# Strassen's seven products for the gate projections of a two-block kernel, with x loaded a second time

## The chip, the cores and the metric

The kernel runs on one NeuronCore of a Trainium2 chip. The metric is the device time of one execution in microseconds. PE is the matrix engine, DVE the vector engine, ACT the scalar engine, POOL the general engine (GpSimd), SP the queue that issues most loads.

## The reference, cut to what matters

Two transformer blocks, one after the other, on 512 tokens of width 1024 in float32. The change is in the first:

```python
h = rms_norm(x, norm_mix_pre[l])
proj = h @ w_in[l]
q, k, v, u, gates = jnp.split(proj, splits, axis=-1)
y_a = chunk_band_attention(q, k, v, rel_bias[l]) @ w_attn_out[l]
y_b = multiscale_pool(u, w_pool_group[l], pool_scale[l]) @ w_pool_out[l]
g_a, g_b = jnp.split(jax.nn.sigmoid(gates + b_gate[l]), N_BRANCH, axis=-1)
mix = (g_a * y_a + g_b * y_b) @ w_o[l]
x = x + rms_norm(mix, norm_mix_post[l])
```

`gates` is 512 tokens by 2048, so its transpose is 16 tiles of 128 channels by 512 tokens.

## The kernel before, in words

Everything is held with channels on the 128 partitions and tokens along the free dimension. A float32 product is made of three matrix products of numbers with short mantissas: each operand is split into a high part (`split_hi`, a copy on ACT that rounds) and a low part (`split_lo`, source minus high part, on DVE), and `mm3` (L411) adds high·high, high·low and low·high in one PSUM bank. A 128x512 output over 1024 input channels is 8 such triples, 24 matmuls of 512 columns (`gemm`, L416).

Weights come in a fixed order (`weight_order`, L66). `fetch` (L366) loads one tile from SP, `split_next` (L377) splits it into one of four `whi`/`wlo` buffers, `take` (L406) hands it to the product. The order of all instructions is settled at build time: the class `Issue` (L107) holds an estimate of each engine's time; every operation goes through `Engine` (L231, so all rows of the profile name that line) and is written into its engine's queue when the estimate says that its turn has come. Small tasks (evacuations, softmax steps, splits) are generators that `step` (L191) resumes between two matmuls. On the chip each engine then works through its queue strictly in order.

The part in question runs as follows. `hhi`/`hlo` are the eight split tiles of `x` times `g_mix`; the tiles `xs` of x stay in SBUF for the residual. After q, k and v, attention (`attn_item`, `attn_values`) runs as small tasks between the products of `w_u`, whose four tiles go through `pooling` (L863): DVE and ACT make moving sums, three matmuls `t<-phi,whi`, `t<-plo,whi`, `t<-phi,wlo` follow, and the result is split into `ph`/`pl`. Then for each m of 8 (L931): two gate tiles (`w_g`, 24 matmuls of 512 columns each), `gate` (L908) multiplies by the row norm `rb1` and takes the tanh; the products `pa` and `pb` (`w_ap`, 12 matmuls each) of attention and pooling follow; `mixing` (L915) joins them into `mxh`/`mxl`. `project_norm` (L575) multiplies these by `w_o`, and its `Seam` adds the result to `xs`. PSUM has 3 banks "mm", 2 "s", 3 "t" (L252).

```python
V.tensor_tensor(lo, src, hi.bitcast(F32), op=ALU.subtract)     # split_lo, L356
V.tensor_tensor(t, ps, rb1, op=ALU.mult)                       # gate, L910
V.tensor_tensor(gt[0], gt[0], gt[1], op=ALU.add)               # mixing, L923
```

Of the kernel before, what the change touches and what calls it, by code (L numbers as in the profile page):

```python
# [10 lines left out]
F32R = mybir.dt.float32r  # L11
# [15 lines left out]
BIG = 1e30  # L27
NACT = 75
WBUF = 1088
NS = 4  # L30

UNITS = ["a6", "a10", "a4", "a1", "a8", "a7", "a3", "a5", "a2", "a9", "q1", "v0", "a0", "q0",
# [33 lines left out]
def weight_order():  # L66

    o = []

    def add(name, i=None, a=0, b=None):  # L70
        o.append((name, i, a, b))

    for hp in range(4):
        add("w_qk", 2 * hp)
        add("w_qk", 2 * hp + 1)
        if hp == 0:
            for i in range(4):
                add("w_v", i)
    add("w_pg")
    for i in range(4):  # L80
        add("w_u", i)
    for m in range(KD):
        add("w_g", 2 * m)
        add("w_g", 2 * m + 1)
        add("w_ap", m)
    for m in range(KD):
        add("w_o", m)
    for i in range(2 * MF):
        add("w_up", i)
# [17 lines left out]
class Issue:  # L107
# [11 lines left out]
    @staticmethod  # L119
    def cells(ap):  # L120
        if ap.space == bass.MemoryType.DRAM:
            return (0,)
        w = ap.ap[0][0]
        a = ap.offset % w
        return range(a // 64, (a + sum(max(st, 0) * (n - 1) for st, n in ap.ap[1:])) // 64 + 1)

    def ready(self, *aps):
        t = 0.0
# [108 lines left out]
def kernel(ctx, tc, aps, out, dbg=None):  # L237
# [26 lines left out]
    def wbuf(tag, n):  # L264

        t = wp.tile([P, WBUF], F32R, tag=tag, name=tag, bufs=4)
        return t[:, :n]
# [29 lines left out]
    def grab_now(tag):  # L297
        until(lambda: tokens[tag])
        until(lambda: tokens[tag][0][0] <= iss.now + LEAD)
        return psum(tag)  # L300

    def free(ps):
        tag, b = bank.pop(ps.name)
        tokens[tag].append((iss.mark, b))
        tokens[tag].sort()

    def after(*aps):
        while iss.ready(*aps) > iss.now + LEAD:
            yield
# [44 lines left out]
    def split_lo(src, hi, lo, scale=None):  # L354
        if scale is None:
            V.tensor_tensor(lo, src, hi.bitcast(F32), op=ALU.subtract)  # L356
        else:
            V.scalar_tensor_tensor(lo, src, scale, hi.bitcast(F32), op0=ALU.mult, op1=ALU.subtract)


    plan = weight_order()
    raws, done = [], []
    early = {("w_up", i) for i in range(NS - 1)} | {("w2_a", int(u[1:])) for u in UNITS[:NS - 1]}
    npos = {"fetch": 0, "split": 0, "taken": 0}

    def fetch():  # L366
        if npos["fetch"] == len(plan):
            return
        name, i, a, b = plan[npos["fetch"]]
        npos["fetch"] += 1  # L370
        src = aps[name] if i is None else aps[name][i]
        n = (src.shape[-1] if b is None else b) - a
        raw = wp.tile([P, n], F32, tag="w32", name="w32", bufs=2)
        load(nc.sync, raw, src[:, a:a + n])
        raws.append(((name, i, a, b), raw, n))

    def split_next():  # L377
        while not raws:
            yield
        key, raw, n = raws.pop(0)  # L380
        yield from after(raw)
        if key[:2] in early:
            hi = [act("wh", F32R) for _ in range(2)]
            lo = [act("wl", F32R) for _ in range(2)]
            for i in range(2):
                split_hi(raw[:, 512 * i:512 * i + 512], hi[i])
                yield
                split_lo(raw[:, 512 * i:512 * i + 512], hi[i], lo[i])
        elif key[0] == "w_out" and key[1] < NPART:

            a, b = NFIRST * P, (8 - NFIRST) * P
            keep = act("wk", F32R), act("wk", F32R)
            hi = [wbuf("whi", a), keep[0][:, :b]]
# [5 lines left out]
        else:  # L399
            hi = wbuf("whi", n)  # L400
            lo = wbuf("wlo", n)
            split_hi(raw, hi)
            yield
            split_lo(raw, hi, lo)
        done.append((key, hi, lo))
        fetch()  # L406

    def take(name, i=None, a=0, b=None):
# [3 lines left out]
        until(lambda: done)  # L412
# [424 lines left out]
    for hp in range(4):  # L837
# [7 lines left out]
        if hp == 0:  # L845
# [9 lines left out]
            spawn(attn_scores())  # L855
            spawn(attn_values())


    plh, pll = [None] * 4, [None] * 4
    wg = weights("w_pg")  # L860

    def pooling(g, ps):
        u = act("u")  # L863
        yield from after(ps)
        V.tensor_tensor(u, ps, rb, op=ALU.mult)
        free(ps)
        yield
        win = u
        for i in range(g + 1):
            s = 1 << i  # L870
            nxt = act("win")
# [23 lines left out]
        plh[g], pll[g] = hi, lo  # L895

    for g in range(4):
        w = weights("w_u", g)
# [6 lines left out]

    rb1 = rb

    def gate(t, ps, col):  # L908
        yield from after(ps)
        V.tensor_tensor(t, ps, rb1, op=ALU.mult)  # L910
        free(ps)
        yield
        A.activation(t, t, AF.Tanh, bias=col, scale=0.5)

    def mixing(m, gt, pa, pb):  # L915
        yield from after(pa, *gt)
        V.scalar_tensor_tensor(gt[0], gt[0], 1.0, pa, op0=ALU.add, op1=ALU.mult)
        free(pa)
        yield from after(pb)
        V.scalar_tensor_tensor(gt[1], gt[1], 1.0, pb, op0=ALU.add, op1=ALU.mult)  # L920
        free(pb)
        yield 0
        V.tensor_tensor(gt[0], gt[0], gt[1], op=ALU.add)  # L923
        yield
        hi, lo = act(f"mh{m}", F32R), act(f"ml{m}", F32R)
        split_hi(gt[0], hi, 0.5)
        yield
        split_lo(gt[0], hi, lo, 0.5)
        mxh[m], mxl[m] = hi, lo

    for m in range(KD):  # L931
        gt = []
        for b in range(2):
            w = weights("w_g", 2 * m + b)
            ps = grab_now("mm")
            gemm(ps, w, hhi, hlo)
            t = act("gate")
            spawn(gate(t, ps, hb[:, 8 * b + m:8 * b + m + 1]))
            gt.append(t)
# [6 lines left out]
        spawn(mixing(m, gt, pa, pb))  # L946
    sn = project_norm(lambda m: [(("w_o", m), range(KD))], mxh, mxl, "g_mix_post", 3, "g_ffn")


# [903 lines left out]
```

## Time and profile before

| | |
|---|---|
| time, median of 3 runs (lowest to highest) | 1023.47 us (1023.25 to 1023.51) |
| the profiled execution: its own time, its span | 1022.24 us, 1020.5 us |
| PE busy | 998.9 us, 98% of the span |
| DVE busy | 694.0 us, 68% |
| ACT busy | 495.9 us, 49% |
| POOL busy | 74.8 us, 7% |
| mean granted TensorE clock | 0.994 |
| loads and stores | 97.19 MB, mean 95 GB/s |

The profiled execution took 1.7 us more than its span, and 1.23 us less than the median of the three runs. A busy share says how long an engine had something in work, and matmuls overlap, so PE's share does not say how near PE is to its peak; the distance from one matmul's start to the next does.

### The profile page before, as it was taken

The numbers are of one execution on the slowest core, as the hardware profiler recorded it, in microseconds if no ns is written. First come the engines' busy times: TensorE is split into PE (matmuls) and PEld (weight loads), VectorE is DVE, ScalarE is ACT, GpSimd is POOL, SyncE is SP. The second block draws the span as 40 slices with busy tenths as digits, with TensorE's granted clock in tenths as the row PEclk, the third lists the DMA queues.
The fourth block names the chain that finished last, engine by engine and source line by source line (L and its number), as shares of the span: only waits on it lengthen the run. The fifth ranks groups of instructions, "written<-read, shape, count | busy, mean of one in ns | idle before, by whom it ended". The sixth has DMA issues, their size and how long they took to land.

```text
span 1020.5 us, 15112 instructions
## 1 busy us (share of the span) xinstructions
PE 998.9 (98%) x5718; PEld 845.8 (83%) x5718; DVE 694.0 (68%) x1429; ACT 495.9 (49%) x1032; POOL 74.8 (7%) x146
## 2 busy tenths in 40 slices
PE   8999999999999999999999999999999989999898
PEld 7977678888888888888888888898899978889786
DVE  6688874444348997766776422369885787999972
ACT  6577543233354554344444322244466675575970
POOL 2000000000002100000001000014000450001001
PEclk9999999999999999999999999999999998999999
DMA  7422122232241233222224333331433440114112
GB/s 260 143 73 81 55 83 90 97 103 94 92 128 38 80 107 99 90 101 103 87 100 119 103 89 92 114 104 28 180 101 110 132 94 22 35 43 134 61 63 83
DMA packets 40345, 97.19 MB, mean 95 GB/s; under 512 B 12160, under 2 KB 16528, under 8 KB 40272
## 3 DMA queue, kind: packets, MB, share of 16 engines
q1 hardware_dynamic: 37392, 87.53, 27.1%
q0 software_dynamic: 2736, 8.66, 2.5%
q8 instruction: 45, 0.74, 0.3%
q14 instruction: 28, 0.23, 0.1%
q10 hardware_dynamic: 144, 0.03, 0.0%
HBM read 90.29 MB, written 5.91 MB: 94 GB/s over the span
## 4 chain that ended last, share of the span: by engine, by line
PE 80%; DVE 13%; DMA 3%; ACT 2%; issue 1%; POOL 1%; SPq 0%; DVEq 0%
PE mm L231 71%; PE t L231 5%; PE s L231 3%; DVE nl L231 2%; DVE x L231 2%; DVE wlo L231 1%; DVE f L231 1%; DVE rsq_t L231 1%; DVE e L231 1%; DMA w<-w_up 1%; DMA T<-dx 1%; DMA w<-w_qk 1%; POOL xt L231 1%; DVE acc L231 1%; POOL cb L231 1%
## 5 line engine op out<-in xcount | busy, mean ns | idle before, releaser
L231 DVE TENSOR_TENSOR wlo<-w,whi 128x1024 fp32r<-128x1024 f32 (+4 forms) x153 | 180.6, 1186 | 63.3 <-ACT whi L231 63.2
L231 PE MATMUL mm<-nh,whi 128*128 128x512 f32 x448 | 176.3, 393 | 0.0
L231 PE MATMUL mm<-nh,wlo 128*128 128x512 f32 x448 | 176.0, 393 | 0.0
L231 PE MATMUL mm<-nl,whi 128*128 128x512 f32 x448 | 175.6, 392 | 0.0
L231 ACT ACTIVATE whi<-w 128x1024 fp32r<-128x1024 f32 (+4 forms) x153 | 154.8, 1018 | 42.6 <-DMA w<-w_dn 22.0
L231 PEld LDWEIGHTS mm<-nh,wlo 128*128 128x128 f32 x448 | 84.2, 188 | 17.0
L231 PEld LDWEIGHTS mm<-nh,whi 128*128 128x128 f32 x448 | 84.2, 188 | 16.9 <-issue 0.4
L231 PEld LDWEIGHTS mm<-nl,whi 128*128 128x128 f32 x448 | 84.2, 188 | 16.7
L231 PE MATMUL mm<-l,whi 128*128 128x512 f32 x208 | 82.4, 396 | 0.0
L231 PE MATMUL mm<-h,whi 128*128 128x512 f32 x208 | 82.3, 396 | 0.0
L231 PE MATMUL mm<-h,wlo 128*128 128x512 f32 x208 | 82.3, 395 | 0.0
L231 PE MATMUL mm<-gh,whi 128*128 128x512 f32 (+1 forms) x198 | 72.5, 366 | 0.0
L231 PE MATMUL mm<-gh,wlo 128*128 128x512 f32 (+1 forms) x198 | 72.4, 366 | 0.0
L231 PE MATMUL mm<-gl,whi 128*128 128x512 f32 (+1 forms) x198 | 72.4, 366 | 0.0
L231 ACT ACTIVATE y<-hu,par 128x512 f32<-128x512 f32 x40 | 32.4, 810 | 63.5 <-DVE hu L231 63.5
L231 DVE SCALAR_TENSOR_TENSOR y<-hu,par,y 128x511 f32<-128x511 f32 x80 | 59.9, 749 | 1.4
L231 POOL TENSOR_TENSOR acc<-acc,sq 128x256 f32<-128x256 f32 (+1 forms) x31 | 26.3, 847 | 418.0 <-ACT sq L231 417.9
L231 PE MATMUL mm<-wlo,nh 128*128 128x256 f32 (+1 forms) x192 | 55.5, 289 | 0.0
L231 PE MATMUL mm<-whi,nl 128*128 128x256 f32 (+1 forms) x192 | 55.3, 288 | 0.0
L231 PE MATMUL mm<-whi,nh 128*128 128x256 f32 (+1 forms) x192 | 55.1, 287 | 0.0
L231 DVE TENSOR_TENSOR hu<-mm,nb 128x512 f32<-128x512 f32 x40 | 27.6, 691 | 39.5 <-PE mm L231 39.5
L231 DVE TENSOR_TENSOR acc<-acc,sq 128x512 f32<-128x512 f32 (+1 forms) x21 | 14.3, 683 | 48.7 <-ACT sq L231 48.5
(344 smaller groups left out, 2209.8 us busy)
## 6 DMA issues: line engine op xcount, KB each, us to landing
w<-w_up SPq DMA_DIRECT2D x44, 512.0 KB, 3.5
w<-w_g SPq DMA_DIRECT2D x16, 512.0 KB, 3.5
w<-w_dn SPq DMA_DIRECT2D x16, 448.0 KB, 3.5
w<-w_a SPq DMA_DIRECT2D x12, 512.0 KB, 3.5
w<-w_ap SPq DMA_DIRECT2D x8, 512.0 KB, 3.5
w<-w_o SPq DMA_DIRECT2D x8, 512.0 KB, 3.4
w<-w_dn SPq DMA_DIRECT2D x8, 512.0 KB, 3.6
w<-w_z SPq DMA_DIRECT2D x8, 512.0 KB, 3.8
```

Of the source, the lines that this page charges most:

```text
L231: return f(*args, **kw)
```

## The change

For each m, the two gate tiles (output channels b = 0, 1) and the two halves of the tokens are taken as a 2 by 2 matrix of 128x256 quarters, and the 1024 input channels as two halves of four tiles. Seven products of 12 matmuls of 256 columns (`strassen`) take the place of eight. The operands are sums of quarters:

- of the activations, once: `forms_of` makes T1 to T4 out of x for each of 4 pairs of input tiles: 2 scaled copies on ACT, 4 differences of 128x256 on POOL, then 2 splits of 128x512 (ACT, DVE). It is started as a task after v.
- of the weights, for each m: `split_next` loads four tiles `rw` of 128x512, POOL makes S1, S2, S3 (and later S4) of 128x512, `split_pair` splits seven quarters (ACT, DVE) into halves of the four weight buffers.
- of the products, for each m: `Sums` copies the first out of PSUM on ACT and adds the other six in seven additions of 128x256 on DVE into the tiles C11 to C22, which are the two gate tiles.

The multiplication by `rb1` now reads SBUF in place of PSUM, `mixing` adds on POOL in place of DVE, and x is loaded again into eight tiles from POOL's queue behind the loop, since the first copies' room is used. `cells` follows tiles in pieces of 16 columns in place of 64; `no_slot` keeps at most four weight buffers in use.

```diff
@@ weight_order
     for m in range(KD):
-        add("w_g", 2 * m)
-        add("w_g", 2 * m + 1)
+        add("w_g", 2 * m, "pair", 2 * m + 1)
         add("w_ap", m)
@@
+    def forms_of(forms_, src, hi, lo, scale):
...
+        for j in range(n):
+            x, y, g, gy = src(j), src(j + n), scale(j), scale(j + n)
+            xg, yg, t, u = (act("tf") for _ in range(4))
+            A.activation(xg, x, AF.Copy, scale=g)
+            A.activation(yg, y, AF.Copy, scale=gy)
+            yield
+            t1, t2, t3, t4 = t[:, half], t[:, other], u[:, half], u[:, other]
+            G.tensor_tensor(t1, xg[:, other], xg[:, half], op=ALU.subtract)
+            G.tensor_tensor(t2, yg[:, other], t1, op=ALU.subtract)
+            G.tensor_tensor(t3, yg[:, other], xg[:, other], op=ALU.subtract)
+            G.tensor_tensor(t4, yg[:, half], t2, op=ALU.subtract)
+            yield
+            for src_, names in ((t, ("T1", "T2")), (u, ("T3", "T4"))):
+                th, tl = act("th", F32R), act("tl", F32R)
+                split_hi(src_, th)
+                yield
+                split_lo(src_, th, tl)
...
@@ split_next
+        if key[2] == "pair":
...
+            s1, s2 = act("sw"), act("sw")
+            G.tensor_tensor(s1, b1, b2, op=ALU.add)
+            G.tensor_tensor(s2, s1, a1, op=ALU.subtract)
+            G.tensor_tensor(b1, a1, b1, op=ALU.subtract)
...
+            yield from split_pair(w, a1, a2, b1, b2, s1, s2)
@@
+    def split_pair(w, a1, a2, b1, b2, s1, s2):
...
+        yield from split("A11", a1)
+        yield from split("S2", s2)
+        G.tensor_tensor(s2, a2, s2, op=ALU.subtract)
+        yield from split("S3", b1)
+        yield from split("A12", a2)
+        yield from split("S1", s1)
+        yield from split("A22", b2)
+        yield from split("S4", s2)
+
+    FORM = {"A11": "B11", "S2": "T2", "S3": "T3", "A12": "B21", "S1": "T1", "A22": "T4", "S4": "B22"}
+
+    def strassen(w, forms, tags, out):
+        for (a, b), tag in zip(FORM.items(), tags):
+            until(lambda: a in w and b in forms)
+            (whi, wlo, slot), (xh, xl) = w[a], forms[b]
+            n = len(xh)
+            ps = grab_now(tag)[:, :256]
+            for j in range(n):
+                mm3(ps, whi[:, csl[j]], wlo[:, csl[j]], xh[j], xl[j], j == 0, j == n - 1)
+            slot["left"] -= 1
+            spawn(out(a, ps), True)
@@ Sums
+            V.tensor_tensor(self.t[name], ps, self.t[other], op=ALU.add)
...
+            if a == "A11":
+                A.activation(self.t["m1"], ps, AF.Copy)
+                self.have.add("m1")
+            else:
+                for name, other in {"S2": (("v", "m1"),), "S3": (("a", "v"),), "A12": (("C11", "m1"),),
+                                    "S1": (("w", "v"), ("C22", "a")), "A22": (("C21", "a"),),
+                                    "S4": (("C12", "w"),)}[a]:
+                    yield from self.add(name, ps, other)
@@ mixing
-        V.tensor_tensor(gt[0], gt[0], gt[1], op=ALU.add)
+        G.tensor_tensor(gt[0], gt[0], gt[1], op=ALU.add)
@@
+    def gated(m, gt, gdone):
+        def done(last):
+            t, col = (gt[1], 8 + m) if last == "A22" else (gt[0], m)
+            V.tensor_tensor(t, t, rb1, op=ALU.mult)
+            yield
+            A.activation(t, t, AF.Tanh, bias=hb[:, col:col + 1], scale=0.5)
...
+        strassen(w[0], hforms, ("s", "mm", "s", "mm", "s", "mm", "s"), Sums(*gt, gated(m, gt, gdone)).out)
...
+    xs[:] = [act(f"x{k}") for k in range(KD)]
+    for k in range(KD):
+        load(nc.gpsimd, xs[k], aps["xT"][k])
```

What the change moves in the queues stands in three places. POOL, from the last loads of attention's bias `rel` on (`acc<-acc,sq` belongs to the norm after `w_o`); before:

```order
L281 DMA rel_977<-rel 128x512
L281 DMA rel_979<-rel 128x512
L281 DMA rel_1211<-rel 128x512
L231 TENSOR_TENSOR acc_2788<-acc_2788,sq_2874 128x256
L231 TENSOR_TENSOR acc_2788<-acc_2788,sq_2890 128x256
```

and with the change, from the last difference of the third pair of input tiles on (`tf` are the tiles of `forms_of`, `rw` loaded and `sw` summed weights):

```order
L232 TENSOR_TENSOR tf_1430<-tf_1428,tf_1427 128x256
L232 TENSOR_TENSOR tf_1430<-tf_1428,tf_1429 128x256
L232 TENSOR_TENSOR sw_1463<-rw_1202,rw_1204 128x512
L232 TENSOR_TENSOR sw_1464<-sw_1463,rw_1198 128x512
L232 TENSOR_TENSOR rw_1202<-rw_1198,rw_1202 128x512
L232 TENSOR_TENSOR tf_1527<-tf_1525 128x256
L232 TENSOR_TENSOR tf_1527<-tf_1526,tf_1527 128x256
L232 TENSOR_TENSOR tf_1528<-tf_1526,tf_1525 128x256
L232 TENSOR_TENSOR tf_1528<-tf_1526,tf_1527 128x256
L232 TENSOR_TENSOR sw_1464<-rw_1200,sw_1464 128x512
```

Between the loads of `rel` and the norm's sums there were no entries; now there are 16 sums of 256 columns and 40 of 512. The weights of the first pair are summed between the third and the fourth pair of input tiles.

PE, at the matmuls of the last of the four `pooling` tasks (`t<-phi` and `t<-plo`); before they stand inside the second gate product:

```order
L231 MATMUL mm_1633<-l_137,whi 128x512
L231 MATMUL mm_1633<-h_129,wlo 128x512
L231 MATMUL t_1661<-phi,whi 128x512
L231 MATMUL t_1661<-plo,whi 128x512
L231 MATMUL t_1661<-phi,wlo 128x512
L231 MATMUL mm_1633<-h_130,whi 128x512
L231 MATMUL mm_1633<-l_138,whi 128x512
```

and with the change behind the seventh product of the first pair (`s_1804`), ahead of the attention product (`ah`):

```order
L232 MATMUL s_1804<-h_132,whi 128x256
L232 MATMUL s_1804<-l_140,whi 128x256
L232 MATMUL s_1804<-h_132,wlo 128x256
L232 MATMUL t_1833<-phi,whi 128x512
L232 MATMUL t_1833<-plo,whi 128x512
L232 MATMUL t_1833<-phi,wlo 128x512
L232 MATMUL mm_1845<-ah_921,whi 128x512
```

The three matmuls have moved from among the gate's own matmuls to the place behind all of them.

DVE, at the `plo` that these wait for; before (`gate<-mm_1575` is the first gate's multiplication by `nb`):

```order
L231 SCALAR_TENSOR_TENSOR pooled<-win,u 128x512
L231 TENSOR_TENSOR pooled<-win,cst 128x16
L231 TENSOR_TENSOR pooled<-pooled,u 128x16
L231 TENSOR_TENSOR gate<-mm_1575,nb 128x512
L231 TENSOR_TENSOR wlo<-w_1532,whi 128x1024
L231 TENSOR_TENSOR plo<-pooled,phi 128x512
L231 SCALAR_TENSOR_TENSOR pl_1668<-t_1661,par,ph_1667 128x512
```

and with the change (`mv`, `av` hold the sums of products; `gate<-s_1804,av` is C12, the sum with the seventh product):

```order
L232 SCALAR_TENSOR_TENSOR pooled<-win,u 128x512
L232 TENSOR_TENSOR pooled<-win,cst 128x16
L232 TENSOR_TENSOR pooled<-pooled,u 128x16
L232 TENSOR_TENSOR gate<-mm_1777,av 128x256
L232 TENSOR_TENSOR wlo<-sw,whi 128x512
L232 TENSOR_TENSOR gate<-s_1804,av 128x256
L232 TENSOR_TENSOR gate<-gate,nb 128x512
L232 TENSOR_TENSOR plo<-pooled,phi 128x512
L232 TENSOR_TENSOR wlo<-rw,whi 128x512
L232 TENSOR_TENSOR gate<-gate,nb 128x512
L232 SCALAR_TENSOR_TENSOR pl_1838<-t_1833,par,ph_1837 128x512
```

`plo` stood behind an entry that needs the first gate product alone; it stands now behind the one that needs the seventh product and a multiplication by `nb`.

In DVE's queue, counted from the last `qk<-mm,nb` (96.52 us in the trace before) to the low half of S3, which the third product needs, there are now eight entries `tl<-tf,th` of 512 columns and the low half of S3 itself more than up to the last `u<-mm,nb` (135.32 us) before; the halves for A11 and S2 stand where one `wlo` of 1024 columns stood. Behind S3, up to the `plo` above, 22 entries follow.

## Rows read from the trace of the kernel before

**Rows 1.** The page: engines over the span (busy us, share, instructions).

```profile
PE 998.9 (98%) x5718; PEld 845.8 (83%) x5718; DVE 694.0 (68%) x1429; ACT 495.9 (49%) x1032; POOL 74.8 (7%) x146
```

**Rows 2.** Windows 96.52:135.92, a later pair 239.20:255.52; columns are named.

```profile
core 0: us, PE busy (x) PEld busy (x) DVE busy (x) ACT busy (x) POOL busy (x), PEclk, DMA share, GB/s
96.52:135.92 39.40, 39.18 (x198) 26.80 (x198) 32.72 (x73) 22.36 (x51) 0.00 (x0) 1.00 0.22 68
239.20:255.52 16.32, 16.32 (x74) 13.52 (x73) 7.46 (x9) 4.93 (x6) 0.00 (x0) 1.00 0.29 98
```

**Rows 3.** Timeline of PE: start us, us, engine line op; 512 columns, gate products.

```profile
135.12 0.39 PE L231 MATMUL mm<-h,whi 128*128 128x512 f32 x1
...
152.80 0.39 PE L231 MATMUL mm<-h,whi 128*128 128x512 f32 x1
...
163.68 0.39 PE L231 MATMUL mm<-ah,whi 128*128 128x512 f32 x1
```

**Rows 4.** Timeline of PE: 256 columns, the first and the one behind 116 of them.

```profile
30.36 0.28 PE L231 MATMUL mm<-whi,l 128*128 128x256 f32 x1
...
44.28 0.40 PE L231 MATMUL mm<-h,whi 128*128 128x512 f32 x1
```

**Rows 5.** Timeline of DVE: starts of entries that follow without a wait.

```profile
345.37 1.23 DVE L231 TENSOR_TENSOR wlo<-w,whi 128x1024 fp32r<-128x1024 f32 x1 [1.47 <-ACT whi L231]
346.51 0.68 DVE L231 TENSOR_TENSOR r<-mm,nb 128x512 f32<-128x512 f32 x1
347.11 1.28 DVE L231 TENSOR_TENSOR r<-s,nb 128x512 f32<-128x512 f32 x2
...
327.29 0.42 DVE L231 TENSOR_TENSOR x<-x,f 128x256 f32<-128x256 f32 x1
327.63 0.41 DVE L231 TENSOR_TENSOR f<-f,t 128x256 f32<-128x256 f32 x1
```

**Rows 6.** Groups of DVE in 309:342, one shape each: xcount, busy us, mean ns.

```profile
L231 DVE SCALAR_TENSOR_TENSOR nl<-x,par,nh 128x256 fp32r<-128x256 f32 x16 | 10.9, 689 | 0.0
L231 DVE TENSOR_TENSOR x<-x,f 128x256 f32<-128x256 f32 x16 | 8.4, 526 | 0.6
L231 DVE TENSOR_TENSOR f<-f,t 128x256 f32<-128x256 f32 x16 | 6.6, 412 | 1.2 <-PE t L231 1.0
```

**Rows 7.** Groups of POOL over the span, one shape each.

```profile
L231 POOL TENSOR_TENSOR acc<-acc,sq 128x256 f32<-128x256 f32 x28 | 21.9, 782 | 400.7 <-ACT sq L231 400.7
L1660 POOL DMA_DIRECT2D x<-x x8 | 4.3, 546 | 0.0
```

**Rows 8.** Timeline: POOL and DVE at the same time.

```profile
17.78 1.29 POOL L231 TENSOR_TENSOR acc<-acc,sq 128x512 f32<-128x512 f32 x1 [16.51 <-ACT sq L231]
...
319.26 0.79 POOL L231 TENSOR_TENSOR acc<-acc,sq 128x256 f32<-128x256 f32 x1 [1.27 <-ACT sq L231]
...
319.37 0.96 DVE L231 SCALAR_TENSOR_TENSOR nl<-x,par,nh 128x256 fp32r<-128x256 f32 x1
...
322.12 0.47 DVE L231 SCALAR_TENSOR_TENSOR nl<-x,par,nh 128x256 fp32r<-128x256 f32 x1
```

**Rows 9.** Timeline of DVE: the last u ahead of the gates.

```profile
135.32 0.69 DVE L231 TENSOR_TENSOR u<-mm,nb 128x512 f32<-128x512 f32 x1
```

**Rows 10.** Timeline: the end of the gates, and PE's first use of them.

```profile
270.43 0.69 DVE L231 SCALAR_TENSOR_TENSOR ml<-gate,mh 128x512 fp32r<-128x512 f32 x1 [0.70 <-ACT mh L231]
...
272.03 0.39 PE L231 MATMUL mm<-ml,whi 128*128 128x512 f32 x1
```

**Rows 11.** Timeline of PE and windows: the longest wait, and the clock behind it.

```profile
841.71 2.46 PE L231 MATMUL s<-cst,T 64*64 64x64 f32 x32 [3.58 <-DMA T<-dx]
...
842.00:844.00 2.00, 1.95 (x32) 1.78 (x30) 0.00 (x0) 0.38 (x1) 0.00 (x0) 0.50 0.05 8
846.00:848.00 2.00, 2.00 (x13) 1.88 (x12) 0.69 (x1) 0.00 (x0) 0.00 (x0) 0.60 0.00 0
848.00:850.00 2.00, 2.00 (x51) 1.73 (x50) 1.87 (x4) 0.86 (x3) 0.00 (x0) 1.00 0.00 0
```

More of the change, by code (lines that the diff above doesn't have):

```diff
@@ L29 @@
 WBUF = 1088
+QOFF = 16
 NS = 4
@@ L124, in cells @@
         a = ap.offset % w
-        return range(a // 64, (a + sum(max(st, 0) * (n - 1) for st, n in ap.ap[1:])) // 64 + 1)
+        return range(a // 16, (a + sum(max(st, 0) * (n - 1) for st, n in ap.ap[1:])) // 16 + 1)
     def ready(self, *aps):
@@ L358, in split_lo, with no_slot @@
             V.scalar_tensor_tensor(lo, src, scale, hi.bitcast(F32), op0=ALU.mult, op1=ALU.subtract)
+    def forms_of(forms_, src, hi, lo, scale):
+        forms = {n: ([], []) for n in ("B11", "B21", "B22", "T1", "T2", "T3", "T4")}
+        half, other = slice(0, 256), slice(256, 512)
+        n = len(hi) // 2
+        for parts, out in ((hi, 0), (lo, 1)):
+            forms["B11"][out].extend(t[:, half] for t in parts[:n])
+            forms["B21"][out].extend(t[:, half] for t in parts[n:])
+            forms["B22"][out].extend(t[:, other] for t in parts[n:])
+        for j in range(n):
[15 more added lines that the diff above has]
+                split_lo(src_, th, tl)
+                yield 0
+                for name, sl in zip(names, (half, other)):
+                    forms[name][0].append(th[:, sl])
+                    forms[name][1].append(tl[:, sl])
+            yield from room()
+        forms_.update(forms)
     plan = weight_order()
     raws, done = [], []
+    slots, slot_of, last = [], {}, [None]
+    def no_slot():
+        return sum(s["left"] > 0 for s in slots) >= 4
     early = {("w_up", i) for i in range(NS - 1)} | {("w2_a", int(u[1:])) for u in UNITS[:NS - 1]}
@@ L370, in fetch @@
         npos["fetch"] += 1
+        if a == "pair":
+            raw = []
+            for t in (i, b):
+                for h in range(2):
+                    raw.append(act("rw"))
+                    load(nc.sync, raw[-1], aps[name][t, :, 512 * h:512 * h + 512])
+            raws.append(((name, i, a, b), raw, 0))
+            return
         src = aps[name] if i is None else aps[name][i]
@@ L380, in split_next @@
         key, raw, n = raws.pop(0)
+        slot = []
+        done.append(slot)
+        if key[2] == "pair":
+            w = {}
+            slot += key, w, None
+            a1, a2, b1, b2 = raw
+            yield from after(*raw)
+            s1, s2 = act("sw"), act("sw")
+            G.tensor_tensor(s1, b1, b2, op=ALU.add)
+            G.tensor_tensor(s2, s1, a1, op=ALU.subtract)
+            G.tensor_tensor(b1, a1, b1, op=ALU.subtract)
+            while quarter["busy"]:
+                yield
+            quarter["busy"] = True
+            yield from split_pair(w, a1, a2, b1, b2, s1, s2)
+            quarter["busy"] = False
+            fetch()
+            return
         yield from after(raw)
@@ L399, in split_next @@
         else:
+            while no_slot():
+                yield
+            slots.append({"left": 1 if key[0] in ("w_pg", "w_u", "w_ap") else 0})
+            slot_of[key] = slots[-1]
             hi = wbuf("whi", n)
@@ L404, in split_next, with qbuf @@
             split_lo(raw, hi, lo)
-        done.append((key, hi, lo))
+        slot += key, hi, lo
         fetch()
+    quarter = {"n": 0, "busy": False}
+    def qbuf():
+        if quarter["n"] % 2 == 0:
+            while no_slot():
+                yield
+            slots.append({"left": 2})
+            quarter["tiles"] = wbuf("whi", WBUF), wbuf("wlo", WBUF)
+        o = QOFF + 512 * (quarter["n"] % 2)
+        quarter["n"] += 1
+        return tuple(t[:, o:o + 512] for t in quarter["tiles"]) + (slots[-1],)
@@ new lines, in split_pair, with split @@
+    def split_pair(w, a1, a2, b1, b2, s1, s2):
+        def split(name, src):
+            yield from after(src)
+            hi, lo, slot = yield from qbuf()
+            split_hi(src, hi)
+            yield
+            split_lo(src, hi, lo)
+            w[name] = hi, lo, slot
+        yield from split("A11", a1)
[6 more added lines that the diff above has]
+        yield from split("S4", s2)
@@ new lines, with __init__, add, out @@
+    class Sums:
+        def __init__(self, ta, tb, done):
+            self.t = {"C11": ta[:, HALF[0]], "C12": ta[:, HALF[1]], "C21": tb[:, HALF[0]], "C22": tb[:, HALF[1]]}
+            mv, av = act("mv"), act("av")
+            self.t.update(m1=mv[:, HALF[0]], v=mv[:, HALF[1]], a=av[:, HALF[0]], w=av[:, HALF[1]])
+            self.have, self.done = set(), done
+        def add(self, name, ps, other):
+            while other not in self.have:
+                yield
+            yield from after(self.t[other])
+            V.tensor_tensor(self.t[name], ps, self.t[other], op=ALU.add)
+            self.have.add(name)
+        def out(self, a, ps):
+            yield from after(ps)
+            if a == "A11":
[6 more added lines that the diff above has]
+                    yield from self.add(name, ps, other)
+            free(ps)
+            yield
+            tile_ = {"A22": ("C21", "C22"), "S4": ("C11", "C12")}.get(a)
+            if tile_:
+                while not self.have.issuperset(tile_):
+                    yield
+                yield from self.done(a)
@@ L411, in take @@
         npos["taken"] += 1
-        until(lambda: done)
+        if last[0] in slot_of and last[0][0] != "w_pg":
+            slot_of[last[0]]["left"] = 0
+        last[0] = name, i, a, b
+        until(lambda: done and done[0])
         key, hi, lo = done.pop(0)
@@ L895, in pooling @@
         plh[g], pll[g] = hi, lo
+        if all(x is not None for x in pll):
+            slot_of["w_pg", None, 0, None]["left"] = 0
     for g in range(4):
@@ L906, with mixing @@
     rb1 = rb
[L908 to L915, printed above, removed]
+    def mixing(m, gt, gdone, pa, pb):
+        while len(gdone) < 2:
+            yield
         yield from after(pa, *gt)
@@ L929, in mixing @@
         mxh[m], mxl[m] = hi, lo
-    for m in range(KD):
[L932 to L939, printed above, removed]
+    def gated(m, gt, gdone):
+        def done(last):
+            t, col = (gt[1], 8 + m) if last == "A22" else (gt[0], m)
+            V.tensor_tensor(t, t, rb1, op=ALU.mult)
+            yield
+            A.activation(t, t, AF.Tanh, bias=hb[:, col:col + 1], scale=0.5)
+            gdone.append(m)
+        return done
+    for m in range(KD):
+        gt = [act("gate") for _ in range(2)]
+        gdone = []
+        w = weights("w_g", 2 * m, "pair", 2 * m + 1)
+        strassen(w[0], hforms, ("s", "mm", "s", "mm", "s", "mm", "s"), Sums(*gt, gated(m, gt, gdone)).out)
         until(lambda: all(x is not None for x in attl + pll))
@@ L945 @@
         gemm(pb, (whi[:, 512:], wlo[:, 512:]), plh, pll)
-        spawn(mixing(m, gt, pa, pb))
+        spawn(mixing(m, gt, gdone, pa, pb))
+    xs[:] = [act(f"x{k}") for k in range(KD)]
+    for k in range(KD):
+        load(nc.gpsimd, xs[k], aps["xT"][k])
     sn = project_norm(lambda m: [(("w_o", m), range(KD))], mxh, mxl, "g_mix_post", 3, "g_ffn")
```

2 lines of the change are left out of this document (added).

## Prediction

> **What bounds the kernel now.** I read the page first: PE is busy 98% of the span, DVE 68%, POOL 7% [rows 1]. So only work taken from PE, or waits given to it, can move the time. Next the windows of the stage: in the 16.32 us of a later gate pair PE never rests and DVE is busy 7.5 us, less than half; but in the 39.4 us ahead of the gates, where attention and pooling run, DVE is busy 32.7 us and rests 6.7 [rows 2]. The gate loop has a vector engine to spare; the stretch before it hardly has. Last I read the timelines for the prices of single entries.
>
> **What PE gains.** A gate pair is 48 matmuls of 512 columns. From 152.80 to 163.68 us they take 10.88 us, 0.227 each [rows 3]. The change makes 7 x 12 = 84 matmuls of 256 columns. Such matmuls, with new weights each time as here, run 0.120 us apart: 116 of them from 30.36 to 44.28 us [rows 4]. 84 x 0.120 = 10.08 us, so a pair saves 0.80 us and eight pairs **6.4 us**. Note how little that is: an eighth fewer columns would be 1.36 us a pair, but the 256-column form loses 0.0066 us per matmul (0.120 against half of 0.227), 84 times.
>
> **What DVE gets.** An entry of 1024 columns holds DVE for 1.14 us up to the next start, one of 512 for 0.60, one of 256 for 0.34 [rows 5]. A pair now costs: 7 low halves of weights, 2 multiplications by the norm, 2 entries of `mixing` and 1 `ml`, 12 x 0.60; 7 additions, 7 x 0.34; the `w_ap` tile 1.14; together 10.7 us of a pair's new 15.52 (10.08 and the unchanged 5.44 of `pa` and `pb`). That fits.
>
> **What POOL does to DVE.** POOL was idle in this part; now it gets 16 sums of 256 columns and 40 of 512. The traced ones take 0.78 us with 256 columns [rows 7] and 1.29 with 512 [rows 8]. They don't run beside DVE for nothing. At 319.26 us POOL starts a sum; DVE's `nl`, which reads two SBUF tiles, starts at 319.37 and takes 0.96 us where 0.47 is usual (322.12): it ends 0.28 us after the sum [rows 8]. Entries that read one operand from PSUM don't suffer: `f<-f,t` has a mean of 412 ns, like its single rows [rows 5, 6]. How much of POOL's time lands on DVE is read from the norm after `w_o`: `nl` is 0.22 us longer than alone (16 times), `x` 0.11 (16 times) [rows 5, 6, 8], 5.3 us in all, against 14 sums of 0.78 us, 11 us: **half of POOL's time**. In the new stretch about six tenths of DVE's time are entries with two SBUF operands (weight halves, `tl`, `win`, `pooled`), as in that norm, so I take a half.
>
> The Trainium skill ("SBUF — State Buffer", section "SBUF: two separate sides") calls this an exclusive lock: the one that starts first holds the shared ports for its whole instruction, and a DVE entry with two SBUF inputs blocks fully. The two rows at 319 us agree. Taken alone the rule would charge every sum in full wherever DVE has such an entry waiting; that is the second rival.
>
> **When the third product can start.** PE gets to the gates at 135.12 us [rows 3]. With the change three `pooling` matmuls (3 x 0.227) stand there, then two products (24 x 0.120) and two matmuls of the third: its low weights (S3) are needed at 138.9 us. DVE before ends the last `u` at 135.9, its start of 135.32 and 0.60 [rows 9]. To this come eight `tl` (4.8 us), the half for S3 (0.6) and POOL's sums up to here, 16 x 0.78 + 3 x 1.29 = 16.4 us, half of it on DVE: 8.2. Of DVE's 6.7 us of rest some are waits for PE and ACT that stay; I give back half, 3.3 (bounds 0 and 6.7). 135.9 + 4.8 + 0.6 + 8.2 - 3.3 = 146.2, so PE waits **7.3 us** (in pieces, at the attention and pooling entries on the way). If POOL's share is 0.3 it is 4.0, at 0.7 10.6.
>
> **Then the pooling matmul.** `t<-plo` now stands behind the seventh product. Unhindered PE would want it 7.2 us after S3 (58 matmuls of 0.120, the rest of the third product and four more, and one of 0.227). DVE has 22 entries between: 12 of 0.60, 7 of 0.34, the `pooled` group of 1.0 us, 10.6 in all, and 3 sums of the next pair on POOL, half of 3.9. 10.6 + 1.9 - 7.2 = **5.3 us** (bounds: 1.5 if DVE is in step, where only C12, the multiplication and `plo` lie behind the seventh product, 0.34 + 0.60 + 0.60; 7.3 if POOL's sums cost all).
>
> **The loop, and its end.** In the loop half of five sums of 1.29 us makes DVE 13.9 of 15.52 us: no wait that lasts, as the weights are split about a pair ahead. At the end the sum of `mixing` goes to POOL behind a `wlo` of 1.14 us. Before, `ml` ended at 271.1 us and was needed at 272.0 [rows 10]; the longer sum uses that up. 0.3 us (0 to 2).
>
> **What I cost at nothing.** ACT gets eight copies and eight splits more ahead of the gates, some 7 us at the mean of its entries there (22.36 us over 51) beside 22 of 39 busy [rows 2]; in the loop it has time. Loading x again is 2 MB and eight issues of 0.55 us on POOL [rows 7], ahead of its last `mixing` sum; the norm that uses x begins behind 309 us [rows 6], 37 after the loop's end, and while they are issued PE has `pa` and `pb` to do. If they waited for their tiles until the end, the last sum would come up to 4.4 us late; that is in the upper bound.
>
> **Sum.** -6.4 + 7.3 + 5.3 + 0.3 = +6.5 us. On the profiled execution that is 1022.24 + 6.5 = 1028.7; that execution was 1.23 us below the median of the runs, so against the median **1030.0 us**.
>
> **Rivals.** *The sums hide* (faster). If POOL's sums fall into DVE's rests or beside its PSUM entries, DVE reaches S3 at 135.9 + 5.4 - 6.7 = 134.6, in time; PE waits 1.5 to 3.4 us at `plo` (10.6 - 7.2), and the time is 1019 to 1021. For it: 6.7 us of rest are there, and a third or more of DVE's entries read PSUM. Against: those rests stand mostly behind PE and ACT. The point from which it decides: with half of the rest given back, PE's waits are 2.8 us plus 20.3 (16.4 and 3.9) times POOL's share, so the change gains below a share of about a sixth, (6.4 - 2.8) / 20.3.
>
> *Full blocking* (slower by far). If each sum costs DVE its whole length, the two waits are 15.5 and 7.3 us, and DVE needs 17.1 us of 15.52 in the loop, 1.6 more in up to seven pairs: 1040 to 1051 us. Against it: the norm shows half. It is what the rule of the Trainium skill named above gives where no PSUM entries lie between.
>
> *The clock.* At 841.71 us PE waited 3.58 us in one piece, and from 842 us its granted clock was 0.50, the lower of the two levels, 1.2 GHz; between 846 and 848 the mean was 0.60, from 848 it was full again [rows 11]. Half a clock for 4 us and 0.40 less for 2 lose 2.8 us. If PE's waits before the gates come in one such piece, that is added: 1033.
>
> *The products don't gain.* At 0.1295 us per matmul 84 of them would cost what 48 did. With 116 at 0.120 in a row I give this next to nothing.
>
> **Chances.** The forecast (share 0.3 to 0.7, rests as bounded) 0.60, its own range 1025 to 1035.5; sums hidden 0.22; full blocking or a lower clock on top 0.11; in between, close to no change, 0.07. Below 0.2% (2.05 us) this kernel's measurement tells no difference: faster 0.23, the same 0.09, slower 0.68. The range leaves out the fastest end of the first rival and most of the second: 1019 to 1036.5.
>
> **What would show it.** Right: matmuls of the gates 0.120 us apart; between 100 and 160 us PE rests 10 to 15 us, released by DVE (`plo`, `wlo`, `tl`), most at `t<-plo`; `tl`, `wlo`, `win` well above 0.69 us there; POOL's sums busy 85 us or so more; the loop from the second pair at 15.5 us a pair. Wrong: DVE entries at their lengths alone and PE without a rest before the gates (first rival); a loop at 16 us a pair or more with PE waiting for `wlo` (second); gate matmuls further than 0.125 us apart.

## The result: 1036.6 us, and the profile after

The changed kernel takes 1036.61 us (median of 4 runs, 1034.98 to 1037.85), the kernel before beside it 1023.36 us (1022.71 to 1023.51). The ratio is 1.013, 95% interval 1.0112 to 1.0147: **13 us slower**, twice the 6.5 us of the forecast and just above the range's upper end, 1036.5. The profiled execution took 1035.93 us (its span 1034.2), 13.7 more than the one shown of before.

The page's line of engines after answers to [rows 1]:

```profile
PE 997.5 (96%) x6006; PEld 854.4 (83%) x6006; DVE 754.8 (73%) x1526; ACT 522.3 (51%) x1095; POOL 158.0 (15%) x210
```

POOL has 83 us more work, DVE 61; PE's share fell from 98 to 96%. PE's timeline shows where the time lies: the first matmul of the first pair, the beginnings of its third and fourth products, the second pair, and `w_o`.

```profile
144.70 0.28 PE L232 MATMUL s<-h,whi 128*128 128x256 f32 x1
146.07 0.28 PE L232 MATMUL mm<-th,whi 128*128 128x256 f32 x1
147.44 0.28 PE L232 MATMUL s<-th,whi 128*128 128x256 f32 x1
...
166.97 0.28 PE L232 MATMUL s<-h,whi 128*128 128x256 f32 x1
...
280.28 0.39 PE L232 MATMUL mm<-mh,whi 128*128 128x512 f32 x1
```

Twelve matmuls from 146.07 to 147.44 us are 0.114 us apart. The third pair begins at 182.33, 15.36 us behind the second. With the other starts read in the same way (us):

| | gates begin | first pair | the other seven | `w_o` begins |
|---|---|---|---|---|
| before | 135.12 | 17.68, with two pooling products of 0.68 | 16.32 each | 267.04 |
| after | 144.70 | 22.27, with one (the other stands ahead) | 15.36, 15.36, 15.36, 16.50, 15.36, 17.80, 17.57 | 280.28 |

`w_o` starts 13.24 us later; behind it hardly anything changes (13.7 in all). A pair without a wait is 0.96 us shorter than before, 7.7 us in eight. So some 21 us are lost, 8.9 ahead of the gates (9.58 less the pooling product that moved there), 6.2 in the first pair (22.27 - 15.36 - 0.68), 5.8 in three of the last four pairs. The list of PE's waits from 90 to 284 us (engine, tile and releaser: us in total, times, longest) has 12.4 us, where before it had 0.2:

```profile
PE s L232 <- DVE wlo L232: 4.5, 4, 2.2
PE t L232 <- ACT phi L232: 4.1, 2, 3.0
PE t L232 <- DVE plo L232: 2.6, 2, 2.3
```

The longest of them, ahead of the second and of the fourth pooling product, in PE's timeline, with the two matmuls that end the slow stretches behind them:

```profile
130.56 0.76 PE L232 MATMUL t<-phi,whi 128*128 128x512 f32 x1 [3.02 <-ACT phi L232]
131.67 0.79 PE L232 MATMUL t<-plo,whi 128*128 128x512 f32 x1 [0.35 <-DVE plo L232]
...
136.85 0.40 PE L232 MATMUL mm<-h,whi 128*128 128x512 f32 x1
...
155.47 0.50 PE L232 MATMUL t<-phi,whi 128*128 128x512 f32 x1 [1.07 <-ACT phi L232]
158.23 0.79 PE L232 MATMUL t<-plo,whi 128*128 128x512 f32 x1 [2.26 <-DVE plo L232]
...
164.24 0.40 PE L232 MATMUL mm<-ph,whi 128*128 128x512 f32 x1
```

A 512-column matmul that ran 0.39 us long in [rows 3] is 0.76 and 0.79 here. The windows show why (the third number from the end is the granted clock):

```profile
130.00:132.00 2.00, 1.09 (x2) 0.62 (x3) 2.00 (x4) 2.00 (x4) 0.47 (x1) 0.50 0.52 211
136.00:138.00 2.00, 2.00 (x9) 1.58 (x8) 2.00 (x4) 0.99 (x3) 0.00 (x0) 0.81 0.00 0
158.00:160.00 2.00, 1.77 (x4) 1.49 (x5) 1.38 (x3) 0.84 (x2) 0.00 (x0) 0.50 0.25 84
```

Behind each of the two waits the clock was granted at 0.50, the lower of its levels, 1.2 GHz, for some 6 us, as in [rows 11]; in the kernel before the mean from 96 to 284 us was 1.00.

And here is what DVE did meanwhile, its timeline ahead of the first of these waits:

```profile
123.91 1.77 DVE L232 TENSOR_TENSOR win<-win 128x510 f32<-128x510 f32 x1
125.61 1.78 DVE L232 TENSOR_TENSOR tl<-tf,th 128x512 fp32r<-128x512 f32 x1
127.31 1.21 DVE L232 SCALAR_TENSOR_TENSOR pooled<-win,u 128x512 f32<-128x512 f32 x1
```

beside POOL's:

```profile
123.52 1.61 POOL L232 TENSOR_TENSOR sw<-sw,rw 128x512 f32<-128x512 f32 x1
125.10 1.74 POOL L232 TENSOR_TENSOR rw<-rw 128x512 f32<-128x512 f32 x1
```

`win` and `tl` of 512 columns, 0.68 and 0.69 us by their means where no sum runs (the run without sums below), take 1.77 and 1.78, and each ends some 0.55 us behind a sum of POOL. The `pooled` that follows is what `phi` is made of. So the wait for `phi`, which the list puts down to ACT, is one for DVE: ACT itself had waited for `pooled`.

```profile
129.85 0.63 ACT L232 ACTIVATE phi<-pooled 128x512 fp32r<-128x512 f32 x1 [4.04 <-DVE pooled L232]
```

By groups of one shape from 96 to 284 us (xcount, busy us, mean ns), DVE:

```profile
L232 DVE TENSOR_TENSOR wlo<-sw,whi 128x512 fp32r<-128x512 f32 x24 | 22.5, 937 | 0.9 <-ACT whi L232 0.9
L232 DVE TENSOR_TENSOR tl<-tf,th 128x512 fp32r<-128x512 f32 x8 | 7.7, 964 | 0.0
L232 DVE TENSOR_TENSOR av<-s,mv 128x256 f32<-128x256 f32 x16 | 6.6, 411 | 0.3 <-PE s L232 0.3
```

and POOL:

```profile
L232 POOL TENSOR_TENSOR tf<-tf 128x256 f32<-128x256 f32 x16 | 15.4, 980 | 50.9 <-ACT tf L232 40.4 <-PE t L232 10.2
L232 POOL TENSOR_TENSOR rw<-rw 128x512 f32<-128x512 f32 x8 | 14.0, 1750 | 0.0
```

Low halves of 512 columns take 0.94 us and more, where one alone takes 0.69, and POOL's sums too are longer than alone, 0.98 us where [rows 7] has 0.78, and the difference `rw` 1.75 where [rows 8] has 1.29. The additions with a PSUM operand (`av<-s,mv`) kept the 0.41 of their size.

### The profile page after: what moved, and what is told of

Its sections match the earlier page's. It is cut to its first block, busy times and chain, and to the rows that moved or that the text cites. A ratio compares the mean times of both kernels' runs of the same rounds, so it can differ in the third digit from the quotient of the medians.

```text
span 1034.2 us, 16013 instructions
## 1 busy us (share of the span) xinstructions
PE 997.5 (96%) x6006; PEld 854.4 (83%) x6006; DVE 754.8 (73%) x1526; ACT 522.3 (51%) x1095; POOL 158.0 (15%) x210
## 4 chain that ended last, share of the span: by engine, by line
PE 70%; DVE 19%; issue 4%; DMA 3%; ACT 2%; POOL 2%; SPq 0%; DVEq 0%; POOLq 0%
PE mm L232 60%; PE s L232 5%; PE t L232 4%; DVE wlo L232 3%; DVE nl L232 2%; DVE e L232 2%; DVE x L232 1%; DVE f L232 1%; DVE rsq_t L232 1%; POOL cb L232 1%; DMA w<-w_a 1%; ACT whi L232 1%; DVE tl L232 1%; ACT e L232 1%; DMA w<-w_qk 1%
## 5 line engine op out<-in xcount | busy, mean ns | idle before, releaser
L232 DVE TENSOR_TENSOR wlo<-w,whi 128x1024 fp32r<-128x1024 f32 (+3 forms) x137 | 162.6, 1193 | 66.8 <-ACT whi L232 66.8
L232 ACT ACTIVATE whi<-w 128x1024 fp32r<-128x1024 f32 (+3 forms) x137 | 138.0, 1014 | 45.8 <-DMA w<-w_dn 21.9
L232 PEld LDWEIGHTS mm<-gl,whi 128*128 128x128 f32 x198 | 37.3, 189 | 6.1
L232 PEld LDWEIGHTS mm<-gh,whi 128*128 128x128 f32 x198 | 37.3, 189 | 6.0
L232 PEld LDWEIGHTS mm<-gh,wlo 128*128 128x128 f32 x198 | 37.3, 189 | 6.0
```

What stands on the lines that cost most here:

```text
L232: return f(*args, **kw)
```

## The experiments

Theory A: POOL's sums hold DVE's entries up, so DVE reaches what PE needs too late. Theory B: DVE is not slowed, the sums themselves come late. Theory C: DVE has too many entries of its own. The time of the kernel before was 1021.2 to 1022.5 us in the median in these comparisons, so ratios to it are compared.

**The sums left out.** In `forms_of`, `split_next`, `split_pair` and `mixing` each sum is still entered in the planner's account but not issued, and the splits read tiles that are there:

```diff
-            G.tensor_tensor(t1, xg[:, other], xg[:, half], op=ALU.subtract)
+            iss.issue("G", "tensor_tensor", [t1], [xg[:, other], xg[:, half]])
-                split_hi(src_, th)
+                split_hi(src_, th, real=xg)
```

> All 64 entries of POOL's new work (16 differences of activations, 32 sums of weights, 8 sums of mixing) are left out, their consumers read tiles that are there anyway; the order of the entries on PE, DVE and ACT is that of the changed kernel, entry for entry, so only POOL's work is gone (the output is not the reference's). Theory A, POOL's sums hold DVE's entries up: 1019 to 1022 us, PE's waits before and in the gates (12.2 us in the changed kernel) fall under 3 us, and no half clock. Theory B, POOL's sums are late themselves and DVE is not slowed: also 1019 to 1022. Theory C, DVE has too many entries of its own: 1030 us or more, with the waits at the pooling matmuls still there.

(The text counts 64 sums; they are 56, 16 + 32 + 8.) Ratio 0.9992 (0.9971 to 1.0013), 1021.22 us, as expected. Two other parts of the expectation were missed: PE's waits from 90 to 284 us are 4.3 us and not under 3, and there is half clock, behind the waits at the fourth pooling product:

```profile
149.75 0.79 PE L233 MATMUL t<-plo,whi 128*128 128x512 f32 x1 [1.30 <-DVE plo L233]
...
150.00:152.00 2.00, 2.00 (x5) 1.57 (x6) 1.17 (x3) 0.99 (x2) 0.00 (x0) 0.50 0.00 0
```

**The sums done for nobody.** The same, but POOL issues all 56, with results that nothing reads:

```diff
+            nc.gpsimd.tensor_tensor(t1, xg[:, other], xg[:, half], op=ALU.subtract)
```

> As the run without the sums, and the same order, but POOL does all 64 sums, of the same sizes, into tiles that nobody reads: they hold ports, and nobody waits for their results (the output is not the reference's). Theory A (DVE is held up beside a sum): 1031 to 1038 us, tl and wlo means near the 0.94 us of the changed kernel, waits of PE again. Theory B (the sums' own lateness): 1019 to 1022 us as without them.

Ratio 1.0164 (1.0135 to 1.0192), 1037.32 us. The low halves of the summed quarters without the sums:

```profile
L368 DVE TENSOR_TENSOR wlo<-rw,whi 128x512 fp32r<-128x512 f32 x24 | 16.4, 685 | 2.5 <-ACT whi L353 2.5
```

and with the dead ones:

```profile
L368 DVE TENSOR_TENSOR wlo<-rw,whi 128x512 fp32r<-128x512 f32 x24 | 23.4, 973 | 1.5 <-ACT whi L353 1.5
```

The two programs differ in POOL's queue alone, DVE does the same 1526 entries, and no entry of PE, DVE or ACT waits for a sum. Only the loads do, for tiles that a sum still reads, and ACT waits for a load 2.0 us with the sums and 1.8 without. So the 16 us between the two runs are what POOL's work does to DVE's, with the half clock that follows: theory A, and B falls. The pages give the size, without the sums

```profile
PE 991.6 (98%) x6006; PEld 851.5 (84%) x6006; DVE 728.1 (72%) x1526; ACT 521.1 (51%) x1095; POOL 78.8 (8%) x154
```

and with the dead ones

```profile
PE 999.7 (97%) x6006; PEld 855.7 (83%) x6006; DVE 757.3 (73%) x1526; ACT 521.5 (50%) x1095; POOL 159.6 (15%) x210
```

DVE is busy 29.2 us longer for 80.8 us of POOL, or for 64.1 us at the lengths these sums have alone (16 x 0.78 and 40 x 1.29): a share of 0.46. The run without sums is not faster than before either, though its products are: 2.4 us of wait at the fourth pooling product remain, 1.0 us for a `wlo` in the last pair, and its first pair still takes 19.91 us. By the starts of the pairs and of `w_o` it loses 6.4 of the changed kernel's 21 us. That part is not from POOL's sums. The waits left are for `phi`, `plo` and low halves, which points to DVE's own entries and the new place of `plo`: theory C in part.

**PE kept busy in the waits.** 12 matmuls of 512 columns more in `pooling`, ahead of the second and fourth product:

```diff
+        if g in (1, 3):
+            for i in range(12):
+                nc.tensor.matmul(ps, wg[0][:, csl[g]], hhi[0], start=True, stop=True)
```

> The changed kernel with 12 matmuls of 512 columns more (2.7 us at full clock) into the same bank ahead of the second and of the fourth pooling product, where PE waited 3.4 and 3.3 us; all else in the same order. If the half clock behind these two waits is a cost of its own (0.5 for some 7 and 6 us): the clock stays full and the time falls by 4 to 7 us, to 1030 to 1033. If not: 1036 to 1038, and if the waits were not real idle time, 1042.

Ratio 1.0163 (1.0133 to 1.0193), 1037.55 us: no gain, where 1030 to 1033 was expected if the half clock can be had back. PE's timeline (the filling rows are `t<-h,whi`):

```profile
129.96 4.62 PE L1045 MATMUL t<-h,whi 128*128 128x512 f32 x12 [2.93 <-DVE et L232]
134.41 0.39 PE L232 MATMUL t<-phi,whi 128*128 128x512 f32 x1
...
137.39 0.39 PE L232 MATMUL mm<-h,whi 128*128 128x512 f32 x1
...
154.97 2.91 PE L1045 MATMUL t<-h,whi 128*128 128x512 f32 x12
157.72 0.39 PE L232 MATMUL t<-phi,whi 128*128 128x512 f32 x1
159.00 0.50 PE L232 MATMUL t<-plo,whi 128*128 128x512 f32 x1 [0.90 <-DVE plo L232]
...
162.31 0.39 PE L232 MATMUL mm<-ph,whi 128*128 128x512 f32 x1
```

At the first place the filling itself waited until 129.96 us, since its bank was held by a transpose, and then ran at a granted clock of 0.58 and 0.56. At the second it did its work, and there the clock stayed full. That gives the price in place: from `t<-plo` to the first `mm<-ph` the same matmuls take 3.31 us here (159.00 to 162.31) and 6.01 in the changed kernel (158.23 to 164.24), 2.7 us. At the first place full clock came earlier: from `t<-phi` 2.98 us (134.41 to 137.39) against 6.29 less a wait of 0.35, 3.0 us. But the total did not fall: behind a wait of 2.2 us in the last pair, which had cost no clock in the changed kernel, this profile has half clock. **Filled otherwise**, with the changed kernel once more beside it: zeros added to the bank that is open at the first place.

```diff
+        if g == 1:
+            for i in range(52):
+                nc.tensor.matmul(run[-1][0][:, :128], run[-1][1], none, start=False, stop=False)
```

> The changed kernel once more, as a measure beside the three others on the same chip: 1034 to 1038 us, waits of PE of about 12 us and two stretches at half clock as in its first profile.

> The changed kernel with PE kept busy in the two long waits ahead of pooling products: 52 matmuls of 128 columns of zeros, added to the bank that is open anyway, ahead of the second pooling product (in the run before, the filling matmuls of that place waited for a bank themselves), and 13 of 512 columns ahead of the fourth, as there; DVE, ACT and POOL in the same order. If the half clock behind the waits is a cost of its own, 2.7 us each (as the second place showed in the run before): 4 to 6 us less than the changed kernel beside it. If the time is set by DVE alone: the same within 1 us.

The changed kernel: 1036.11 us, ratio 1.0136 (1.0113 to 1.0159). Filled: 1035.17 us, ratio 1.0127 (1.0103 to 1.0151), the same by the medians. Its six executions lie apart: three took 1033.3 to 1033.4 us with a mean clock of 0.995, three 1036.9 to 1040.8 with 0.990 to 0.992, and the profile is of the slowest, 1040.78. The clock's windows of that profile:

```profile
144.00:148.00 4.00, 3.62 (x10) 2.14 (x11) 1.59 (x3) 1.38 (x3) 0.00 (x0) 0.59 0.00 0
272.00:276.00 4.00, 4.00 (x27) 4.00 (x27) 1.87 (x4) 0.89 (x1) 0.80 (x2) 0.70 0.91 331
```

Again it fell elsewhere, behind the wait of the third pooling product and in the last pair. So the half clock costs what the timelines show, but the medians don't show that it can be had back while the waits remain; the three short executions of the last run leave it open. A wait of 2.21 us in the last pair was followed by a clock of 1.00 in the changed kernel and by half clock in the run before; on what that hangs stays open.

**All sums on DVE.** `G.` to `V.` in the nine lines that sum:

```diff
-            G.tensor_tensor(s1, b1, b2, op=ALU.add)
+            V.tensor_tensor(s1, b1, b2, op=ALU.add)
```

> All 64 sums on DVE in place of POOL (0.34 us for 256 columns, 0.60 for 512; 13.7 us of DVE's work in a pair of 15.52). Theory A: DVE loses less to its own sums than to POOL's: 1024 to 1030 us, tl and wlo back at 0.69 us. Theory C (DVE is simply full): 1038 us or more, with longer waits for plo and wlo.

1030.05 us, ratio 1.0094 (1.0068 to 1.012): about 4 us better than on POOL by the ratios, at the edge of what theory A gave. The low halves are back at 0.68 us. The order of the entries is another, since it is settled at build time from each engine's account. What remains are waits of another kind, the longest of them:

```profile
PE t L232 <- DVE plo L232: 4.4, 1, 4.4
PE t L232 <- DVE pl L232: 3.1, 1, 3.1
PE s L232 <- DVE wlo L232: 2.2, 1, 2.2
```

The first two stand in the attention and pooling stretch, where DVE hardly rested before [rows 2] and now has forms and sums as well. The third stands in the sixth pair, which took 19.20 us with the half clock behind it; there five of DVE's own sums of 512 columns stand in a row, from 226.15 to 229.4 us, ahead of the `wlo` that PE waits for until 230.03. That is theory C at these places: the work is pressed into the wrong place.

**The first pair made as before, forms made beside it.** `weight_order` and the loop over m:

```diff
+        if m < NC:
+            add("w_g", 2 * m)
+            add("w_g", 2 * m + 1)
...
+        if m < NC:
+            gt = []
+            for b in range(2):
+                w = weights("w_g", 2 * m + b)
+                ps = grab_now("mm")
+                gemm(ps, w, hhi, hlo)
...
+GATES = 0.0, 1.6
...
+    iss.pe = 1.04
```

with NC = 1, all sums on DVE, and from `w_u` to `w_o` the planner's thresholds LEAD and SLACK set to 0.0 and 1.6 and its PE times 4% longer.

> The first of the eight pairs is made as before (48 matmuls of 512 columns), so that the forms of x are made beside it and the fourth pooling product stands among its matmuls again; all sums on DVE; in the part from w_u to w_o the issue order is planned with PE's times 4% longer and other thresholds. Theory A (waits come from POOL's sums and from work pressed ahead of the first pair): PE's waits there gone, seven pairs of 15.36 us, 6.7 us won: 1016 to 1019 us where the kernel before takes 1023. Theory C (DVE, 13.7 of 15.36 us in a pair, can't keep up): waits for wlo in the pairs, 1023 us or more.

**1019.11 us, ratio 0.9968 (0.9955 to 0.9981): faster than both kernels**, than the one before by 0.3%, at the upper edge of what theory A gave. From the second pair on no pair has a wait; its start, that of the third, and `w_o`:

```profile
156.52 0.28 PE L239 MATMUL s<-h,whi 128*128 128x256 f32 x1
...
171.88 0.28 PE L239 MATMUL s<-h,whi 128*128 128x256 f32 x1
...
264.04 0.39 PE L239 MATMUL mm<-mh,whi 128*128 128x512 f32 x1
```

Seven periods of 15.36 us from 156.52 to 264.04. In [rows 3] the second pair began at 152.80, so 3.7 us of the 6.7 won are spent ahead of it, 2.5 of them waits, most of them for `plo`:

```profile
PE t L239 <- DVE plo L239: 1.8, 2, 0.9
```

Which of its three edits does it? **One plain pair, the sums on POOL**, the changed kernel's planning:

> The first pair made as before, but all sums on POOL as in the change, and the changed kernel's own planning. Theory A: the sums of the forms now fall beside a pair with 8.8 us of rest on DVE, the weight sums hold DVE up in the other seven (5 x 1.3 to 1.75 us of POOL in 15.36): some waits in the loop, 1023 to 1031 us, slower than the run with the sums on DVE by 5 us or more. If it was only the place of the forms and not POOL: 1016 to 1020, like that run.

1035.69 us, ratio 1.0139 (1.0116 to 1.0162): above both ranges, and no better than the changed kernel. The waits moved into the loop. **The same with the sums on DVE:**

> One plain pair and all sums on DVE, with the changed kernel's own planning: it differs from the run with the sums on POOL (1035.7 us) by the engine of the sums alone. Theory A (POOL's sums hold DVE up): 10 us less than that run or better, 1019 to 1025 us, with wlo at 0.68 us. If that run's waits came from planning: 1030 us or more here too.

1023.25 us, ratio 1.0011 (0.9997 to 1.0026), as theory A gave. The engine of the sums, with the order that the planner makes of it, is worth 13 us here by the ratios; the two programs' sources differ in the nine sums alone, but the order of PE's and ACT's entries differs too. On POOL, a group of DVE's low halves and the wait that low halves make:

```profile
L237 DVE TENSOR_TENSOR wlo<-sw,whi 128x512 fp32r<-128x512 f32 x21 | 19.5, 928 | 4.0 <-ACT whi L237 4.0
```

```profile
PE s L237 <- DVE wlo L237: 8.1, 4, 3.0
```

and on DVE:

```profile
L237 DVE TENSOR_TENSOR wlo<-sw,whi 128x512 fp32r<-128x512 f32 x21 | 14.3, 682 | 4.4 <-ACT whi L237 4.4
```

```profile
PE s L237 <- DVE wlo L237: 1.7, 2, 1.5
```

**The kernel before with the new planning alone** (the three planning lines):

> The kernel before, without products of quarters, with only the planning numbers of the fast version in the part from w_u to w_o. If that version's 3.3 us come from the seven products: no change, within 1 us of the kernel before. If from the planning: 2 to 4 us faster.

1024.66 us, ratio 1.0025 (1.001 to 1.004): 0.25% slower, neither of the two outcomes. So the planning by itself wins nothing. But the fast version needs it: with one plain pair and the sums on DVE it is what lies between 1.0011 and 0.9968, some 4 us, and without it that version is no faster than the kernel before. **Eight pairs by quarters with that planning** (NC = 0):

> All eight pairs by products of quarters, all sums on DVE, with the planning of the fast version: it differs from that version by the plain first pair alone. If pressing the forms ahead of the first pair is the remaining cost: waits of 4 us or more ahead of and in the first pair, 1023 to 1029 us. If the planning alone cured it: 0.9 us below the fast version, 1018.

1029.31 us, ratio 1.0066 (1.0047 to 1.0085), just above the first range: all seven later pairs at 15.36, but 8.3 us of waits in the first, the longest of them for `phi`, and behind it

```profile
154.87 0.69 PE L239 MATMUL t<-phi,whi 128*128 128x512 f32 x1 [3.21 <-ACT phi L239]
157.26 0.80 PE L239 MATMUL t<-plo,whi 128*128 128x512 f32 x1 [1.71 <-DVE plo L239]
```

so the plain first pair is worth 10 us. **Two plain pairs** (NC = 2):

> Two plain pairs in place of one, else as the fast version. Six pairs save 5.8 us in place of 6.7; it is slower by 0.96 us if the forms are done in time with one plain pair already, and equal or faster if they still cost PE waits there (2.5 us before the second pair): 1018 to 1020 us.

1019.68 us, ratio 0.998 (0.9966 to 0.9993), by the ratios 1.2 us behind one plain pair. The intervals overlap, so the two are not told apart; a second plain pair brings no gain that shows.

No run has one plain pair and the new planning with the sums on POOL.

## Why the prediction was wrong in size

- **PE's gain** was forecast at 0.80 us a pair and is 0.96. The nearest rows [rows 4] were of a product whose standing operand is the activations, at 0.120 us; the gates' run at 0.114 to 0.118. A row of the same shape was not one of the same use; whether that is the reason no run shows.
- **POOL's share**, a half, was right: 0.46 of the sums' lengths alone, over the whole. The Trainium skill ("SBUF — State Buffer", "SBUF: two separate sides") states an exclusive lock, where the later one blocks fully; the rows at 123.91 and 125.61 us agree, and POOL's longer sums show it from the other side. Over the whole less is charged than that; that it is so because part of the sums falls beside PSUM entries and rests was not measured by itself.
- **Where the waits fall.** Counted waits are 12.2 us above before, forecast 12.9, but that the totals are so near is luck: 4.3 ahead of the gates (7.3 forecast), 3.3 at the fourth pooling product (5.3) and 4.5 in the loop (0.3). The third product, where the forecast put the first wait, never waited. Of the 3.3 at the fourth pooling product 2.4 remain without any sum, so they come from the new place of `plo` more than from POOL. The step that failed in the loop is "13.9 of 15.52 us: no wait that lasts". It looked at the mean of a pair; POOL's sums come in a bunch, and the `wlo` that PE wants falls among them, as here in the fifth pair of the changed kernel:

```profile
217.47 1.62 POOL L232 TENSOR_TENSOR sw<-sw,rw 128x512 f32<-128x512 f32 x1
...
217.86 1.77 DVE L232 TENSOR_TENSOR wlo<-sw,whi 128x512 fp32r<-128x512 f32 x1
...
219.69 0.38 PE L232 MATMUL s<-th,wlo 128*128 128x256 f32 x1 [0.59 <-DVE wlo L232]
```

  The half, 1.77 us beside sums, ends at 219.6, and PE has it at 219.69. Without any sums 1.0 of the loop's 4.5 us remains; with all sums on DVE in a bunch it is 2.2, and in the fast version no pair by quarters waits.
- **The clock** was the failing step of most weight. It stood as a rival of its own, 3 us, once, within a chance of 0.11. It was not a rival but went with the forecast's own waits: 3.4 us of wait in a stretch are near the 3.58 behind which [rows 11] showed half clock. It came twice, 5.7 us by the timelines above, where the sum had nothing.
- The sum then is -7.7 + 12.2 + 5.7 = +10.2, and 3 us to 13.2 are not in the list of waits: a matmul of 256 columns is shown 0.28 us long and the next starts 0.118 behind it, so pauses under 0.16 us, and that much of each longer one, aren't counted. The pair of 16.50 us has 0.59 counted and lost 1.14. For the rest of the 3 us this is argued from that pair.
- **Signs that failed.** Between 100 and 160 us PE rests 7.9 us by the list, not 10 to 15, and more of it at `phi` (4.1) than at `plo` (2.6). The gates' matmuls are 0.114 to 0.118 us apart, not 0.120, and a pair without a wait takes 15.36 us, not 15.5.
- **Right:** the direction, and of its mechanism that DVE is held up by POOL's sums and reaches `pooled`, `plo` and the low halves too late (halves at 0.94 us and more, POOL's 83 us). ACT and the second load of x cost nothing that the rows show: PE does not wait for `ml` ahead of `w_o`.

## What to carry to other kernels

An idle POOL is no free engine beside a DVE that reads two SBUF tiles: a 512-column sum that DVE itself does in 0.60 us took POOL up to 1.75 us, and about half of POOL's time was added to DVE's. A reform of operands that saves PE 6% of a stage must be paid where DVE has rest: here that meant giving up the saving in one round of the loop and making the forms beside it, with the sums on DVE and the order planned anew, and it won 0.3%. And if the forecast has PE wait for 2 to 3 us, give the half clock behind the wait a term in the sum, with a chance: here it came behind some such waits and not behind others.

## What the runs showed of the hardware that was not expected

That DVE and POOL lengthen each other, both: 0.68 to 0.94 us and 1.29 to as much as 1.75 us by the means of their groups. And that filling PE's waits moved the half clock to other waits rather than ending it, in the executions that were profiled. No length of a wait told the two cases apart: in the run with one plain pair and the sums on POOL a wait of 2.95 us (to 213.69) was followed by a granted clock of 0.50 from 214 to 218 us, one of 2.97 (to 251.95) by 1.00 up to 258.
